# A hybrid decoder trunk on one core: the order of its first loads, and the queue of its first half's attention

## The chip, the core and the metric

The kernel runs on one core of a Trainium2 chip. The metric is the device time of one execution in microseconds (us); the median of three runs is taken. PE is the matmul engine (TensorE), DVE VectorE, ACT ScalarE, POOL GpSimd; SP issues nearly all DMAs.

## What is computed

Two layers over 1024 tokens of width 1024, float32. In each, a normalised input goes through one wide product, whose columns feed three groups: sparse attention (an indexer scores all causal keys, the 256 best per query stay), a conv module and a pool. Then an output product, an MLP of width 4096 with a squared ReLU, and a per-layer embedding behind a gate:

```python
a = rmsnorm(h, norm_mix_pre[i])
u = jnp.einsum('bsd,de->bse', a, w_in[i])
q, k, v, qi, ki, wi, u_conv, u_pool = jnp.split(u, IN_SPLITS, axis=-1)
...
mix = jnp.concatenate([y_attn, y_conv, y_pool], axis=-1)
mix = jnp.einsum('bse,ed->bsd', mix, w_out[i])
h = h + rmsnorm(mix, norm_mix_post[i])
m = rmsnorm(h, norm_mlp_pre[i])
m = jnp.square(jax.nn.relu(jnp.einsum('bsd,df->bsf', m, w_up[i])))
m = jnp.einsum('bsf,fd->bsd', m, w_down[i])
h = h + rmsnorm(m, norm_mlp_post[i])
gate = jax.nn.sigmoid(jnp.einsum('bsd,de->bse', h, ple_gate[i]))
h = h + gate * jnp.einsum('bsp,pd->bsd', p[i], ple_proj[i])
```

## The kernel before

Tokens are cut into two halves of 512, channels lie on the 128 partitions. The program goes through eight phases, for layer 0: the input product ("win") of the first half, win of the second, the rest ("m", `m_phase`) of the first half; then layer 1's win of the first half, layer 0's m of the second, and so on.

**Dense work.** A unit is one 128x512 output tile: eight input tiles by three matmuls, since float32 operands are split into a rounded part (hi) and its rest (lo): hi by hi (L255), hi by lo (L260), lo by hi (L261; a unit that goes first on new tiles has L257 and L258). Weights come by `weights` and `prepare` in the order of the list `coming`: a load of 512 KB by SP into wraw (two buffers, L211), ACT makes whi (L216), POOL wlo (L217). A unit's sums lie in pd (three buffers in PSUM) and are evacuated by ACT or DVE: L390 in win, L985 for the first four input tiles' worth of the first m.

**The start.** `first_x` (L1080 loads, L277 to L297) loads x and splits it into scaled hi and lo tiles on ACT and DVE, and squares it; the squares go through L319 (PE column sums), L347 (a power on POOL) and L324 (PE spreads the norm's factor, rb). `rope_tables` loads positions and constants, makes the rope tables on DVE and ACT, and sends them through DRAM. `first_x` of the second half runs at its own place in win of the first half, and its loads go into the buffer yT that the first half's x has used. The conv module's 31 taps are DVE steps of L586.

**Attention.** It is a generator that `run` advances between dense units, by a budget per phase. For a pair of heads and a block of 128 queries: PE scores (L647), DVE bias and maximum (L816), ACT exponential with its sum (L825), DVE reciprocal (L826), ACT scale (L827); then PE transposes (L839), ACT and DVE split the result (L272, L273), PE multiplies with the values (L847, L848), and `finish` (L853 to L862) stores into mixS in DRAM. `attend` keeps one group of heads ahead: a group's softmax is issued before the group ahead of it is weighted. The first half's blocks 2 and 3 take their tiles from the ring `rows`.

**The first half's m in layer 0** needs mixS whole. So its output product is in two parts: the four tiles of conv and pool first (L982 to L986), and when attention is through (`drain`), the four attention tiles (loaded at L970). A norm (`post_norm`: L319, L347, L324, then L925 and L926 for each tile, and new splits) leaves PE without tiles; it takes a filler, a part of the embedding's product (`embedding`, L954, evacuated at L956). The norm after the output product fills with output tiles 4 to 7, which are stored to DRAM (eS), and the norm after the MLP with tiles 0 to 3, which stay in SBUF for the gate.

A scheduler puts the instructions of each engine in order when the program is built, so a change in the code moves rows that it doesn't name. Engines run in order.

## Time and profile before

| | us |
|---|---|
| median of three runs | 2783.4 (2782.57 to 2784.98) |
| profiled execution | 2778.56 |
| its span in the trace | 2776.8 |
| PE busy | 2685.9 (97%) |
| DVE, ACT, POOL busy | 1660.4, 1588.5, 1348.8 |
| mean granted clock of PE | 0.994 |

All sums below stand against the profiled execution. PE is nearly always busy, so the stretches to look at are those in which it isn't: windows of the trace give them. A granted clock of 1.00 is 2.4 GHz, the higher of PE's two levels; a mean of 0.79 over a stretch is part of it at the lower, 1.2 GHz.

### The profile page before, as it was taken

To read this page: it belongs to the slowest core of one execution; us is meant where nothing else is said; L and a number is where in the kernel's file an instruction comes from. 1 tells how busy PE (TensorE), PEld (TensorE's weight loads), DVE (VectorE), ACT (ScalarE), POOL (GpSimd) and SP (SyncE) were. 2 spreads that over 40 slices of the span, in tenths; PEclk is the share of its full clock that TensorE was granted. 3 is DMA by queue.
4 is the path that set the end of the run, shared out by engine and by line. 5 is a ranking of instruction groups with operands and counts; after the bars stand their busy time and mean duration, and the time that the engine had idled before them with its cause. 6 is when DMAs were issued, how large, how long until landed. Compare 5 with 4: busy or idle time off the path is not lost.

```text
span 2776.8 us, 37158 instructions
## 1 busy us (share of the span) xinstructions
PE 2685.9 (97%) x12496; PEld 2210.5 (80%) x12496; DVE 1660.4 (60%) x3393; ACT 1588.5 (57%) x2971; POOL 1348.8 (49%) x1073
## 2 busy tenths in 40 slices
PE   8899999999999999999999999999999999999998
PEld 6778778887888777788888778788878887788886
DVE  6978578678557868784522585676785662311123
ACT  5357767766767434684733434677657764443343
POOL 4654334444334664544344765444443345544446
PEclk9999999999999999999999999999999999999999
DMA  5677554432344555644233646534222454422323
GB/s 183 199 196 220 134 165 120 107 99 84 88 110 124 195 188 186 183 122 118 90 100 109 222 141 222 158 97 112 98 88 84 103 185 152 141 94 96 99 95 132
DMA packets 192022, 377.41 MB, mean 136 GB/s; under 512 B 17432, under 2 KB 76952, under 8 KB 191832
## 3 DMA queue, kind: packets, MB, share of 16 engines
q1 hardware_dynamic: 130200, 319.46, 36.1%
q0 software_dynamic: 42240, 20.98, 4.6%
q10 hardware_dynamic: 19392, 34.61, 3.6%
q8 instruction: 98, 1.61, 0.2%
q14 instruction: 92, 0.75, 0.1%
HBM read 304.67 MB, written 70.32 MB: 135 GB/s over the span
## 4 chain that ended last, share of the span: by engine, by line
PE 77%; DVE 10%; DMA 6%; issue 2%; ACT 2%; POOL 2%; SPq 0%; ACTq 0%; POOLq 0%; DVEq 0%
PE pd L255 22%; PE pd L261 21%; PE pd L260 21%; PE bank L647 6%; DMA wraw<-win 2%; PE bank L839 2%; DVE bank L586 1%; POOL wlo L217 1%; PE bank L848 1%; PE bank L847 1%; DVE dtmp L925 1%; DVE row L801 1%; DMA kd<-kS 1%; DVE slot L273 1%; PE pd L319 1%
## 5 line engine op out<-in xcount | busy, mean ns | idle before, releaser
L217 POOL TENSOR_TENSOR wlo<-wraw,whi 128x512 fp32r<-128x512 f32 x824 | 1087.9, 1325 | 1211.7 <-ACT whi L216 1162.5
L255 PE MATMUL pd<-slot,whi 128*128 128x512 f32 x3296 | 1300.6, 395 | 38.4 <-ACT whi L216 17.8
L261 PE MATMUL pd<-slot,wlo 128*128 128x512 f32 x3168 | 1239.0, 392 | 12.7 <-POOL wlo L217 12.6
L260 PE MATMUL pd<-slot,whi 128*128 128x512 f32 x3168 | 1240.3, 392 | 0.4 <-DVE slot L278 0.3
L216 ACT ACTIVATE whi<-wraw 128x512 fp32r<-128x512 f32 x824 | 511.8, 628 | 767.3 <-PE pd L260 536.9
L255 PEld LDWEIGHTS pd<-slot,whi 128*128 128x128 f32 x3296 | 621.4, 189 | 177.1 <-ACT whi L216 22.2
L261 PEld LDWEIGHTS pd<-slot,wlo 128*128 128x128 f32 x3168 | 597.1, 188 | 139.7 <-POOL wlo L217 17.2
L260 PEld LDWEIGHTS pd<-slot,whi 128*128 128x128 f32 x3168 | 597.6, 189 | 119.7 <-DVE slot L278 1.2
L647 PE MATMUL bank<-kd,qst 128*128 128x512 f32 (+3 forms) x1024 | 259.1, 359 | 12.9 <-DVE mxc L816 5.0
L695 DVE SCALAR_TENSOR_TENSOR idx<-bank,wiT,idx 128x512 f32<-128x512 f32 (+3 forms) x300 | 187.7, 651 | 66.1 <-ACT bank L691 62.1
L647 PEld LDWEIGHTS bank<-kd,qst 128*128 128x128 f32 x1024 | 176.2, 189 | 48.4 <-DVE idx L695 10.5
L1012 DVE TENSOR_SCALAR pd<-pd 128x512 f32<-128x512 f32 x128 | 88.9, 696 | 170.3 <-PE pd L261 169.2
L691 ACT ACTIVATE bank<-bank 128x512 f32<-128x512 f32 (+2 forms) x320 | 153.2, 506 | 61.2 <-PE bank L647 59.1
L1031 DVE TENSOR_TENSOR yT<-yT,pd 128x512 f32<-128x512 f32 x96 | 65.4, 684 | 201.1 <-PE pd L261 201.0
L718 DVE TENSOR_SCALAR_CACHE_REDUCE row<-row,cc 128x640 f32<-128x640 uint16 (+1 forms) x124 | 133.6, 1078 | 72.2 <-ACT row L732 65.1
L586 DVE SCALAR_TENSOR_TENSOR bank<-win,vec,bank 128x512 f32<-128x512 f32 x232 | 164.3, 747 | 5.8 <-ACT bank L584 4.0
L732 ACT ACTIVATE row<-row,cc 128x768 f32<-128x768 uint16 (+1 forms) x124 | 121.4, 982 | 21.9 <-DVE cc L738 20.5
L273 DVE TENSOR_TENSOR slot<-pd,slot 128x512 fp32r<-128x512 f32 x128 | 87.8, 687 | 69.0 <-ACT slot L272 68.6
L297 DVE TENSOR_TENSOR dtmp<-dtmp,pd 128x512 f32<-128x512 f32 x88 | 60.2, 684 | 105.2 <-ACT pd L293 105.0
L816 DVE CUSTOM_DVE_ANT_0 row<-bank,idx 128x512 f32<-128x512 f32 (+3 forms) x160 | 92.1, 591 | 51.5 <-PE bank L647 38.5
L273 DVE TENSOR_TENSOR cmat<-bank,cmat 128x512 fp32r<-128x512 f32 (+1 forms) x160 | 98.3, 631 | 33.2 <-ACT cmat L272 32.4
L825 ACT ACTIVATE row<-row,nmc,rq 128x384 f32<-128x384 f32 (+5 forms) x96 | 93.0, 969 | 22.7 <-DVE nmc L821 18.4
(218 smaller groups left out, 2635.9 us busy)
## 6 DMA issues: line engine op xcount, KB each, us to landing
wraw<-wup SPq DMA_DIRECT2D x128, 512.0 KB
wraw<-wdown SPq DMA_DIRECT2D x128, 512.0 KB
wraw<-win SPq DMA_DIRECT2D x84, 512.0 KB
qiS<-dtmp ACTq DMA_DIRECT2D x64, 256.0 KB
slot<-mixS SPq DMA_DIRECT2D x32, 512.0 KB
wraw<-wgate SPq DMA_DIRECT2D x32, 512.0 KB
qst<-qiS POOLq DMA_DIRECT2D x48, 256.0 KB, 3.4
hS<-yT SPq DMA_DIRECT2D x48, 256.0 KB
```

Of the source, the lines that this page charges most:

```text
L216: sc.activation(hi, r, AF.Copy)
L217: gp.tensor_tensor(lo, r, hi.bitcast(F32), op=OP.subtract)
L255: te.matmul(ps, wh, xh, start=i == 0, stop=False)
L260: te.matmul(ps, wh, xl, start=False, stop=False)
L261: te.matmul(ps, wl, xh, start=False, stop=i == n - 1)
L273: ve.tensor_tensor(lo, src, hi.bitcast(F32), op=OP.subtract)
L586: ve.scalar_tensor_tensor(acc[:, c] if k == TAPS - 1 else pa, src, w, pa, op0=OP.mult, op1=OP.add)
L647: te.matmul(ps[:, :n1 - n0], q, kd[:, k, k0 + n0:k0 + n1], start=k == 0, stop=k == 1)
L691: sc.activation(r, r, AF.Relu)
L695: ve.scalar_tensor_tensor(at, r, w, at, op0=OP.mult, op1=OP.add)
L718: ve.tensor_scalar(flags[:, :Ws[j]], of[j], t, None, op0=op, op1=OP.add, accum_out=dst[:, j:j + 1])
L732: sc.activation(flags[:, :Ws[j]], of[j], AF.Sign, scale=-1.0, bias=c[:, j:j + 1], accum_out=cnt[:, j:j + 1])
```

## The change

1. **First loads.** The first weights are asked for ahead of the first x tile and the second ahead of the second x tile (before: one, after two x tiles); the constants cv go behind the rope's. For the second half a copy of eight columns of the first half's norm factor into yT is written ahead of its loads, so that they have to wait for it.
2. **Attention queue.** For the first half, blocks 2 and 3 use six tiles instead of rows' own (three of `rows` beside three of `spare`), and two groups are kept ahead instead of one. A generator that finds no free tile now gives way (`take`) instead of failing. In layer 0, block 3's scale goes from ACT to DVE. `drain` advances the other generators where its own gives way.
3. **Embedding.** In layer 0's first half the product of output tiles 0 to 3 (24 matmuls, four evacuations, four stores) stands after the first part of the output product, that is beside the end of attention, instead of in the norm after the MLP, which now has no filler; the gate reads these four tiles from eS, as it does the others.

```diff
@@ -109,6 +109,12 @@
...
+    def take(ring):
+        while not ring.free:
+            yield None
+        return ring.get()
@@ -153,7 +159,6 @@
...
     cv = const.tile([P, 2, 17], F32, name="cv")
-    sy.dma_start(cv, cinv)
     lent = dtmp.get()
@@ -189,6 +194,7 @@
...
         sy.dma_start(fr, invf)
+        sy.dma_start(cv, cinv)
         sy.dma_start(pf.bitcast(I32), at)
@@ -226,13 +232,14 @@
...
             if (l, hf) == (0, 0):
-                coming += [wout[l, o][:, 4:] for o in range(NK)] + [wout[l, o][:, :4] for o in range(NK)]
+                coming += [wout[l, o][:, 4:] for o in range(NK)] + [wple[l, i] for i in range(2)] + [wout[l, o][:, :4] for o in range(NK)]
             else:
                 coming += [wout[l, o] for o in range(NK)]
-            coming += [wple[l, i] for i in range(2, 4)]
+            apart = (l, hf) == (0, 0)
+            coming += [wple[l, i] for i in (range(2, 4) if apart else range(2, 4))]
             for gr in range(4):
                 coming += [wup[l, gr * 8 + u] for u in range(8)] + [wdown[l, gr, o] for o in range(NK)]
-            coming += [wple[l, i] for i in range(2)] + [wgate[l, o] for o in range(NK)]
+            coming += [wple[l, i] for i in (() if apart else range(2))] + [wgate[l, o] for o in range(NK)]
     ready = []
@@ -364,7 +371,7 @@
...
-        rb = rms_sb(sq, keep=rq[:, l, hf, 0])
+        rb = state["rb"] = rms_sb(sq, keep=rq[:, l, hf, 0])
         for i, f in ((1, 0.125), (2, -0.125)):
@@ -573,7 +580,7 @@
...
-        at = rows.get()
+        at = yield from take(rows)
         acc = at[:, :1024].rearrange("p (c t) -> p c t", c=2)
@@ -809,7 +816,7 @@
...
             for g in heads:
-                t = ring.get()
+                t = yield from take(ring)
                 mx, nm, rs, ri = tiny("mx", 2), tiny("nm", 1), tiny("rs", 1), tiny("ri", 1)
@@ -824,7 +831,11 @@
...
                 ve.reciprocal(ri, rs)
-                sc.activation(s, s, AF.Copy, scale=ri)
+                if l == 0 and b == 3:
+                    ve.tensor_scalar(s, s, ri, None, op0=OP.mult)
+                else:
+                    sc.activation(s, s, AF.Copy, scale=ri)
                 out.append(t)
@@ -862,11 +873,11 @@
...
-        def attend(some, at, ring):
+        def attend(some, at, ring, ahead=1):
             n = (some[-1] + 1) * P
-            before = None
-            for step in [(kv, b, g) for kv in range(2) for b in some for g in (0, 2)] + [None]:
+            queue = []
+            for step in [(kv, b, g) for kv in range(2) for b in some for g in (0, 2)] + [None] * ahead:
                 if step:
@@ -877,8 +888,9 @@
...
                         qst.put(q)
-                if before:
-                    (bkv, bb, bg), bpr = before
+                    queue.append((step, pr))
+                if len(queue) > ahead or not step:
+                    (bkv, bb, bg), bpr = queue.pop(0)
                     v0 = 4 * bkv if hf == 0 else 0
@@ -888,14 +900,19 @@
...
                         yield 2.0
-                before = step, pr
...
             yield from together(select(), attend(blocks[:2], (HALF, HALF), ctmp))
-            yield from attend(blocks[2:], (0, HALF), rows)
+            mine = []
+            for _ in range(3):
+                mine.append((yield from take(rows)))
+            spare.put(*mine)
+            yield from attend(blocks[2:], (0, HALF), spare, 2)
+            rows.put(*mine)
         else:
@@ -939,6 +956,8 @@
...
         ts = slice(hf * HALF, hf * HALF + HALF)
+        if not pairs:
+            return lambda: iter([None])
         pl = [slots.get() for _ in range(2)]
@@ -984,6 +1003,9 @@
...
+            for _ in embedding(l, hf, range(2), None)():
+                pass
             load(xs, range(4), ts)
@@ -999,7 +1021,7 @@
...
             yield 5.2
-        fill = embedding(l, hf, range(2, 4), None)
+        fill = embedding(l, hf, range(2, 4) if apart else range(2, 4), None)
         slots.put(*xs)
@@ -1036,7 +1058,7 @@
...
         es = []
-        fill = embedding(l, hf, range(2), es)
+        fill = embedding(l, hf, () if apart else range(2), es)
         xs, _ = post_norm(sqy, vl[:, V_MLP_POST:V_MLP_POST + 8], ts, hS, None, fill, apart2)
@@ -1075,11 +1097,14 @@
...
         xs = []
+        if hf == 1:
+            ve.tensor_copy(yT[:, :, :1], state["rb"][:, :NK].unsqueeze(2))
         for k in range(NK):
             h = yT[:, k]
+            if hf == 0 and k in (0, 1):
+                ready.append(prepare(coming.pop(0)))
             sy.dma_start(h, xT[k * P:(k + 1) * P, ts])
-            if k == 1 and hf == 0:
-                ready.append(prepare(coming.pop(0)))
         for k in range(NK):
@@ -1122,8 +1147,9 @@
...
-        while advance([x for x in bg if x[0] == (l, hf)]) is not None:
-            pass
+        while any(x[0] == (l, hf) for x in bg):
+            if advance([x for x in bg if x[0] == (l, hf)]) is None:
+                assert advance(bg) is not None
```

SP's first instructions, before (vec and cv are constants, yT x, wraw weights):

```order
L154 DMA vec<-vecs 128x204
L156 DMA cv<-cinv 128x34
L1080 DMA yT<-xT 128x512 x2
L211 DMA wraw_91<-win 128x1024
L1080 DMA yT<-xT 128x512 x6
L211 DMA wraw_92<-win 128x1024
L191 DMA fr<-invf 128x2
L513 DMA row_121<-wcp 128x256
L1080 DMA yT<-xT 128x512 x3
L211 DMA wraw_91<-win 128x1024
L1080 DMA yT<-xT 128x512 x4
L192 DMA dtmp_108<-pos 128x1x64
```

and after:

```order
L160 DMA vec<-vecs 128x204
L217 DMA wraw_91<-win 128x1024
L1107 DMA yT<-xT 128x512
L217 DMA wraw_92<-win 128x1024
L1107 DMA yT<-xT 128x512 x7
L196 DMA fr<-invf 128x2
L197 DMA cv<-cinv 128x34
L520 DMA row_121<-wcp 128x256
L217 DMA wraw_91<-win 128x1024
L217 DMA wraw_92<-win 128x1024
L198 DMA dtmp_108<-pos 128x1x64
L210 DMA tabS<-dtmp_108 128x64 x2
L217 DMA wraw_91<-win 128x1024
```

The weights stand behind vec alone, cv behind the x tiles, and of the second half's eight loads (the second mention of yT) the first stands behind five weights and the positions.

ACT around the last evacuations that stand beside attention in the first half's m, before (L985 evacuates the output product, L825 is an exponential, L827 a scale, L272 a split, L856 `finish`):

```order
L216 ACTIVATE whi_96<-wraw_92 128x512
L985 ACTIVATE yT<-pd_139 128x512
L272 ACTIVATE cmat_117<-bank_144 128x512
L272 ACTIVATE cmat_119<-bank_140 128x512
L825 ACTIVATE row_124,rsc_1356<-row_124,nmc_1352,rq 128x384
L825 ACTIVATE row_122,rsc_1357<-row_122,nmc_1353,rq 128x384
L827 ACTIVATE row_124<-row_124,ric_1360 128x384
L272 ACTIVATE cmat_115<-bank_144 128x512
L827 ACTIVATE row_122<-row_122,ric_1361 128x384
L825 ACTIVATE row_121,rsc_1358<-row_121,nmc_1354,rq 128x384
L825 ACTIVATE row_123,rsc_1359<-row_123,nmc_1355,rq 128x384
```

and after (L1004 is the evacuation of before's L985, L975 the embedding's, L832 the exponential, L838 the scale):

```order
L279 ACTIVATE cmat_119<-bank_141 128x512
L832 ACTIVATE row_122,rsc_1359<-row_122,nmc_1355,rq 128x384
L832 ACTIVATE row_121,rsc_1360<-row_121,nmc_1356,rq 128x384
L975 ACTIVATE dtmp_102<-pd_139 128x512
L838 ACTIVATE row_122<-row_122,ric_1363 128x384
L838 ACTIVATE row_121<-row_121,ric_1364 128x384
L222 ACTIVATE whi_94<-wraw_92 128x512
L975 ACTIVATE dtmp_108<-pd_137 128x512
L279 ACTIVATE cmat_115<-bank_140 128x512
L832 ACTIVATE idx_132,rsc_1357<-idx_132,nmc_1353,rq 128x512
L832 ACTIVATE idx_133,rsc_1358<-idx_133,nmc_1354,rq 128x512
L867 ACTIVATE ctmp_113<-bank_142 64x512
```

Before, eight exponentials (four of 384 columns, and four of 512 further on) follow the last L985; after, four of 512 follow the last L975, two of them behind these rows, and no scale of 512 is left on ACT in this place.

PE at the norm after the first half's MLP in layer 0, before (twelve transposes, the filler's first six matmuls, column sums L319, scores L647):

```order
L839 MATMUL bank_141<-ident,row_123 128x128
L255 MATMUL pd_139<-slot_85,whi_95 128x512
L260 MATMUL pd_139<-slot_85,whi_95 128x512
L261 MATMUL pd_139<-slot_85,wlo_99 128x512
L255 MATMUL pd_139<-slot_86,whi_95 128x512
L260 MATMUL pd_139<-slot_86,whi_95 128x512
L261 MATMUL pd_139<-slot_86,wlo_99 128x512
L319 MATMUL pd_138<-ones,dtmp_101 128x1 x4
L647 MATMUL bank_144<-kd,qst_128 128x512 x2
L847 MATMUL bank_142<-cmat_117,vst 128x256
```

and after (L850 is a transpose, L326 the column sums, L654 scores, L858 and L859 the values):

```order
L850 MATMUL bank_141<-ident,row_122 128x128
L850 MATMUL bank_141<-ident,row_121 128x128
L326 MATMUL pd_139<-ones,dtmp_105 128x1 x4
L654 MATMUL bank_144<-kd,qst_128 128x512 x2
L858 MATMUL bank_142<-cmat_117,vst 128x256
L326 MATMUL pd_139<-ones,dtmp_103 128x1 x4
L859 MATMUL bank_142<-cmat_118,vst 128x256
L858 MATMUL bank_142<-cmat_117,vst 128x256
L859 MATMUL bank_142<-cmat_118,vst 128x256
```

The column sums follow the transposes at once; there is no matmul of the embedding here.

## Rows read from the trace of the kernel before

**Rows 1.** The page's busy table: busy us, share of the span, instructions.

```profile
PE 2685.9 (97%) x12496; PEld 2210.5 (80%) x12496; DVE 1660.4 (60%) x3393; ACT 1588.5 (57%) x2971; POOL 1348.8 (49%) x1073
```

**Rows 2.** Windows: busy us of each engine, granted clock, DMA share, GB/s.

```profile
core 0: us, PE busy (x) PEld busy (x) DVE busy (x) ACT busy (x) POOL busy (x), PEclk, DMA share, GB/s
0.00:30.50 30.50, 17.79 (x72) 13.19 (x73) 22.85 (x41) 21.93 (x38) 13.17 (x16) 1.00 0.74 252
...
79.50:141.00 61.50, 53.66 (x230) 42.73 (x229) 57.55 (x80) 25.12 (x45) 40.37 (x33) 0.97 0.61 191
...
270.00:326.30 56.30, 55.28 (x271) 45.81 (x270) 31.70 (x83) 39.21 (x82) 23.79 (x20) 1.00 0.48 131
326.30:351.20 24.90, 19.61 (x103) 16.39 (x102) 15.75 (x47) 21.61 (x46) 2.82 (x3) 0.79 0.59 107
...
842.30:858.80 16.50, 16.50 (x109) 14.97 (x108) 11.57 (x30) 13.73 (x26) 4.94 (x4) 1.00 0.25 80
```

**Rows 3.** Timeline of SP: start us, us, engine, line, operation.

```profile
1.20 0.42 SPq L156 DMA_DIRECT2D cv<-cinv  x1
...
2.60 0.43 SPq L211 DMA_DIRECT2D wraw<-win  x1
```

**Rows 4.** Timeline of PE at the start; in brackets the wait and its releaser.

```profile
9.36 0.79 PE L255 MATMUL pd<-slot,whi 128*128 128x512 f32 x1 [9.36 <-ACT whi L216]
...
28.41 0.51 PE L255 MATMUL pd<-slot,whi 128*128 128x512 f32 x1 [1.85 <-ACT whi L216]
...
30.12 0.50 PE L261 MATMUL pd<-slot,wlo 128*128 128x512 f32 x1 [0.98 <-POOL wlo L217]
```

**Rows 5.** Timeline of DVE, 25 to 50 us.

```profile
27.33 0.74 DVE L278 SCALAR_TENSOR_TENSOR slot<-yT,vec,slot 128x512 fp32r<-128x512 f32 x1
...
48.36 0.70 DVE L390 TENSOR_TENSOR pd<-pd,rb 128x512 f32<-128x512 f32 x1 [6.79 <-PE pd L261]
```

**Rows 6.** Waits of PE, 79 to 141 us: us, times, longest.

```profile
PE pd L261 <- POOL wlo L217: 2.8, 1, 2.8
```

**Rows 7.** Timeline of PE at the end of the first attention.

```profile
326.30 0.28 PE L847 MATMUL bank<-cmat,vst 128*128 128x256 f32 x1
326.42 0.60 PE L839 MATMUL bank<-ident,row 128*128 128x128 f32 x4
326.78 0.36 PE L848 MATMUL bank<-cmat,vst 128*128 128x256 f32 x1
...
343.91 1.54 PE L839 MATMUL bank<-ident,row 128*128 128x128 f32 x6 [1.94 <-ACT row L827]
...
351.15 0.28 PE L848 MATMUL bank<-cmat,vst 128*128 128x256 f32 x1
```

**Rows 8.** Chain of work that ended last, 350 to 364 us.

```profile
358.32 5.10 DMA slot<-mixS
```

**Rows 9.** Groups by line and form: count, busy us, mean ns, idle.

```profile
L956 ACT ACTIVATE dtmp<-pd 128x512 f32<-128x512 f32 x32 | 18.8, 591 | 3.2 <-PE pd L261 3.1
...
L825 ACT ACTIVATE row<-row,nmc,rq 128x512 f32<-128x512 f32 x16 | 12.9, 806 | 0.1
...
L827 ACT ACTIVATE row<-row,ric 128x512 f32<-128x512 f32 x16 | 11.1, 711 | 0.3 <-DVE ric L826 0.2
```

**Rows 10.** Timeline of DVE, the scalar step L800 on 128x512.

```profile
268.18 1.60 DVE L800 TENSOR_SCALAR idx<-idx,thrc 128x512 f32<-128x512 f32 x1
...
1256.63 0.48 DVE L800 TENSOR_SCALAR idx<-idx,thrc 128x512 f32<-128x512 f32 x1
```

**Rows 11.** Timeline of POOL, 262 to 271 us.

```profile
266.96 3.97 POOL L217 TENSOR_TENSOR wlo<-wraw,whi 128x512 fp32r<-128x512 f32 x3 [6.16 <-ACT whi L216]
```

**Rows 12.** Timeline of PE at the norm after the MLP.

```profile
840.73 0.39 PE L261 MATMUL pd<-slot,wlo 128*128 128x512 f32 x1
...
842.09 0.40 PE L261 MATMUL pd<-slot,wlo 128*128 128x512 f32 x1
...
853.52 0.60 PE L324 MATMUL pd<-ident,rrn 128*128 128x128 f32 x4
...
858.84 0.39 PE L255 MATMUL pd<-slot,whi 128*128 128x512 f32 x1
```

## The prediction

> **What bounds the kernel now.** I read the page's busy table first [rows 1]: TensorE (PE) is busy 97% of the span. Dense matmuls stand 0.227 us apart where nothing is in the way (840.73 to 842.09, six steps) [rows 12], so PE time that is really work can't shrink by this change (it has as many matmuls after as before), and time can come only out of the stretches in which PE waits. The windows by stage [rows 2] show where these lie inside the change's reach: the first 30.5 us (PE busy 17.8), 79.5 to 141 (53.7 of 61.5), the end of layer 0's first attention with nothing else left to do, 326.3 to 351.2 (19.6 of 24.9, at a mean granted clock of 0.79). The stretch 842.3 to 858.8, the second norm of the first half, is full (16.5 of 16.5). The change fills the third of these, and takes its filler from the last. The busy shares count overlapping matmuls, so below I count waits by start times: PE work is priced at its undisturbed spacing, 0.2275 us for a dense matmul, and the same for a 512-column L647, 0.36 for four transposes of L839 (326.42 to 326.78), 0.12 for a matmul of L847 or L848 (326.30 to 326.42) [rows 7].
>
> **Part 1, the order of the first loads.** Before, SP issues vec, cv and two of the x tiles ahead of the first weights, which it issues at 2.60 us [rows 3]; ACT turns them into whi, and that releases PE's first matmul at 9.36 [rows 4]. After, the weights stand behind vec alone, where cv stood, at 1.20: 1.4 us earlier, and with 104 + 512 KB ahead of their end instead of 1,145 KB (estimate from the tiles' sizes). I take 1.5 us for the first matmul. The x tiles after it come no later in the list, and ACT sets their pace in both. Further, PE's order now interleaves the first two units tile by tile, so it has 48 dense matmuls to run before it needs the norm, and the third unit's weights are asked for earlier: the waits at 28.41 (1.85 us) and 30.12 (0.98) [rows 4], 2.8 together, lie on the path, since the third unit is next. I take 2.5 of them, so 4.0 for the first 30.5 us, between 1.5 (the first matmul only) and 5.5 (also the time that PE stood in single-column sums of L319).
>
> Held back: a copy of the first half's norm into yT makes the second half's eight loads wait for it. Its price: SP is in order, and behind the waiting load stand the next weights and the rope tables. On DVE six splits of the second half now stand ahead of the evacuation at 48.36; that row waited 6.79 us for PE, and six times 0.74 us is 4.4 [rows 5], so they fit with 2 us to spare. I cost them at nothing; with that cover gone it would be up to 4.4 us of DVE, minus the 2.8 below. Rope's eight small DVE steps now stand ahead of the norm's two, on data whose load is issued behind four of the weights, so this too can be late. These are the reasons for the low end of 1.5.
>
> The conv chain on DVE (L586), whose first step follows the evacuation at 48.36 and the units behind it, begins earlier if the start is 4 us earlier, and of the 7.8 us that PE does not work in 79.5 to 141 [rows 2] (DVE busy 57.6 of 61.5) some 0 to 2.8 us go (2.8: the wait for wlo there [rows 6]); I take 1. Part 1: **5.0**, between 1.5 and 8.3.
>
> **Part 2, the deeper queue and the scale on DVE.** In the tail, from the end of PE's last dense matmul (326.30, the first of the rows) to its last L848 (351.15, so 351.27) there are 102 attention matmuls: 40 L839, 44 of L847/L848, 12 L647 of 512 columns, six shorter. At the spacings above: 3.6 + 5.3 + 2.8 + 0.9 = 12.6. So 12.4 of 25.0 us are waits, and the longest that is named is softmax's: L839 for ACT's scale L827, 1.94 us at 343.91 [rows 7]. Eight heads have their exponential still to come after ACT's last dense evacuation: **1.55 us of wait each**. After, the order puts 24 embedding matmuls ahead of the tail and, by the third group in flight, eight more heads' exponentials ahead of their evacuations: four heads, all of 512, are left. The tail has 90 attention matmuls: 32 L839, 40 L847/L848, 14 L647, 4 short: 2.9 + 4.8 + 3.2 + 0.3 = 11.2. With 4 × 1.55 = 6.2 of waits it lasts 17.4. It begins 24 × 0.2275 = 5.5 and 12.6 − 11.2 = 1.4 later, at 333.2, and ends at 350.6, 0.7 earlier than before, with 5.5 us of dense work done besides: 6.2 in all. From it goes what the four heads cost beside dense work: the dense stretch 270 to 326.3 holds eight heads and lost 2.1 us (its length less the spacings of its 271 matmuls [rows 2]), 0.26 a head, so 1.0. What follows the tail, finish, store and load of mixS (the load 5.10 us [rows 8]), is the same in both, and with it PE's work there on the next index. Part 2: **+5.1**.
>
> Bounds: the four heads' waits may fall to 4 × 0.26 (then part 2 is 12.4 − 1.0 − 1.0 = 10.4), or all twelve last heads may pay 1.55 (below). Engines beside it: ACT was busy 39.2 of 56.3 us in the dense stretch [rows 2]; four more exponentials of 0.81 and four evacuations of 0.59 [rows 9] make 44.8 of 63: enough. The scale of the eight 512-column heads goes from ACT (0.71 [rows 9]) to DVE. No such step of DVE is in the trace; the nearest is L800, a scalar step on 128x512 in SBUF, 0.48 us at 1256.63 and 1.60 at 268.18 [rows 10], where POOL was in three of L217 from 266.96 on [rows 11]. I take 0.6, near the shorter, since POOL has little to do in the tail. DVE was busy 31.7 of 56.3 and 15.8 of 24.9 [rows 2], so it is not the bound, and exponential, reciprocal and scale of one head stay in series: no gain by itself but ACT's 0.71 between two heads.
>
> The Trainium skill, SBUF — State Buffer, section Who interferes with whom, speaks against this move: a tensor_scalar in a two-port mode and GpSimd lock each other out of a shared port pair for a whole instruction, and who issues first wins. The long L800 beside POOL's L217 [rows 10, 11] agrees with it; by the rule at its worst the sum is rival C's, by the shorter row the forecast's.
>
> **Part 3, the norm that loses its filler.** Between the last dense matmul of wdown (842.09) and the first that needs the normalised tiles (858.84) PE ran 24 embedding matmuls, 5.5 us, and 11 us of attention and sums, without a gap [rows 12]. After, the 24 are gone and the order there reads transposes, sums, scores. The norm's chain (L319, POOL's power, L324 at 853.52, L925, L926, splits on DVE) doesn't get shorter by itself: if it takes 16.5 us still, the 5.5 are given back whole. But DVE was busy only 11.6 of the 16.5 [rows 2], and idle for 4.9; with PE's queue shorter, L319 comes 1.4 us sooner at once (six dense matmuls stood ahead of it). I let half of the 4.9 close: cost 5.5 − 2.5 = **3.0**, between 0.6 and 5.5. Four more e tiles now come from DRAM for the gate, loads issued a norm ahead: nothing. [...]
>
> **Sum.** 5.0 + 5.1 − 3.0 = 7.1 us. The profiled run took 2778.56 (span 2776.8) and by that would take 2771.5; it lies 4.8 under the median of the three runs, 2783.4, and I carry the difference to the median: **2776.3**. A measurement of this kernel tells about 0.2%, 5.6 us, from no change, so faster means under 2777.8.
>
> **Rivals.**
> A, the filler was not needed and the tail closes: four heads at 0.26, norm 0.6, start 5.0: 10.4 + 5.0 − 0.6 = 14.8, 2768.6. For it: DVE and ACT have idle time in both. Against it: softmax's steps are in series and the last group has nothing behind it.
> B, given back: the norm costs all of 5.5 and the start brings only 2 (the conv chain on DVE, nearly unbroken, ends when it did): 5.1 + 2 − 5.5 = 1.6, 2781.8. For it: DVE's 57.6 of 61.5 us in 79.5 to 141, and L925/L926 in series behind L324.
> C, the scale on DVE is slow: each stands behind POOL, 1.6 instead of 0.48. Four in the tail are 4.5 us: 7.1 − 4.5 = 2.6, 2780.8. Against it: in the tail POOL is busy 2.8 of 24.9 us [rows 2]. It is the mechanism of the rule that the Trainium skill has in SBUF — State Buffer, section Who interferes with whom.
> D, slower: threading twelve heads' transposes into dense work holds PE, which is in order, at each: 12 × 1.55 = 18.6 of waits instead of 12.4. With the norm's 5.5 and a start of 4: −6.2 − 5.5 + 4 = −7.7, 2791.1. It decides where ACT and DVE can't finish a group's exponentials within the dense matmuls that the order puts between it and its transposes; against it ACT's 44.8 of 63.
> E, the change doesn't do what it says: the held-back loads stall SP and the second half's first units wait, so the start gives nothing; with the rest as forecast 5.1 − 3.0 = 2.1, 2781.3. I count it with B.
>
> **How the numbers follow.** Forecast 0.55, A 0.13, B and E 0.17, C 0.05, D 0.10. The forecast's own range, from the ends that are likely of each term, is 2773 to 2780; four fifths of it lie under 2777.8. Faster: 0.8 × 0.55 + 0.13 = 0.57. Slower: D but for a fifth, 0.08. Same: 0.35. The range that leaves no more than 2 in 10 out takes in A's time, nearly, and B, C and E: 2767 to 2784; D is left out.
>
> **What would show it.** PE's first matmul at about 7.8, and the first matmul on wlo of its third unit by about 26 to 26.5 instead of 30.1; the conv chain's first step some 4 us earlier. The tail 17 us long, from 333 less the start's gain, with no wait above 2 us in the dense stretch before it, and the wait for mixS as long as before. A gap of about 3 us between L319 and the first matmul on normalised tiles in the norm, with L324 less than 11.4 us after the end of wdown. The prediction is wrong if that norm loses 5 us or more, if L839 waits for the scale amid dense matmuls, or if the second half's loads are waited for near 48.

## The result

| | us | |
|---|---|---|
| before, median of 4 runs | 2784.2 | 2782.6 to 2788.8 |
| changed, median of 4 runs | 2770.2 | 2768.9 to 2772.1 |
| ratio | 0.9944 | 95% interval 0.9932 to 0.9956 |
| forecast | 2776.3 | 2767 to 2784 |

The change is 14 us faster (by the interval 12 to 19), twice the 7.1 that the forecast had, and inside its range. A second comparison gave 0.9956 (0.9942 to 0.9970). The profiled execution of the change has a span of 2770.3 us, 6.5 less than that of before (2776.8); which of the two differences is to be believed was the first question for the runs. Three executions that lie far above the others of their kernels (3100, 7788 and 12488 us) are left out of all comparisons. Lines have moved: a dense unit is now L262, L267, L268; whi L222, wlo L223; column sums L326, spread L331; transposes L850, exponential L832, scale L838 and L836, values L858 and L859.

The page of the changed kernel, busy table and chain:

```profile
PE 2685.5 (97%) x12496; PEld 2213.7 (80%) x12496; DVE 1656.6 (60%) x3402; ACT 1584.7 (57%) x2963; POOL 1351.9 (49%) x1073
...
PE 82%; DVE 9%; DMA 4%; issue 2%; ACT 1%; POOL 1%; SPq 0%; ACTq 0%; POOLq 0%; DVEq 0%
```

PE's work is what it was [rows 1]; its waits are less. To see where, I took from each trace the time from every PE matmul's start to the next one's, less the median spacing of its form, and summed these waits over stretches cut at equal amounts of PE work. The stretches are named by their times in the profile of before. Two profiles stand for each kernel, the second ones from the runs below; the last column compares the means.

| stretch, us | what | before, twice | changed, twice | waits saved |
|---|---|---|---|---|
| 0 to 136 | start and first units | 28.0, 26.8 | 27.3, 28.3 | −0.4 |
| 136 to 283 | rest of both halves' win, layer 0 | 6.5, 7.0 | 4.8, 5.0 | 1.9 |
| 283 to 417 | end of the first attention | 22.4, 22.8 | 18.1, 18.1 | 4.5 |
| 417 to 854 | MLP | 7.0, 7.1 | 7.3, 6.9 | 0 |
| 854 to 929 | norm and gate | 4.9, 5.1 | 4.3, 4.3 | 0.7 |
| 929 to 1084 | first half's win, layer 1 | 14.7, 16.4 | 11.0, 9.5 | 5.3 |
| 1084 to end | the rest | 58.7, 58.6 | 63.3, 62.2 | −4.1 |

Down to 1084 us the change saves 12.0 us. Behind that it loses 4.1 in the profiles. PE's order differs from that of before only up to 1399 us, and the loss lies behind it, among rows that stand in the same order; this last stretch lost 58.0 to 63.3 us in the kernels of this study. The 1.9 us of 136 to 283 are no firmer: the other kernels made from the change lose 5.6 to 8.2 there. I don't put these 4.1 us down to the change; why the stretch differs so stays open. What is left by the profiles is 7.9 us, and why the medians of the plain runs lie 14 us apart stays open too.

**The start.** PE at the start of the changed kernel (start us, us, engine, line; in brackets the wait and its releaser):

```profile
7.30 0.79 PE L262 MATMUL pd<-slot,whi 128*128 128x512 f32 x1 [7.30 <-ACT slot L284]
...
25.36 0.75 PE L331 MATMUL pd<-ident,rq 128*128 128x128 f32 x4 [2.13 <-POOL rq L354]
27.88 0.80 PE L262 MATMUL pd<-slot,whi 128*128 128x512 f32 x1 [1.76 <-DVE dtmp L280]
28.47 0.63 PE L267 MATMUL pd<-slot,whi 128*128 128x512 f32 x1
28.89 0.63 PE L268 MATMUL pd<-slot,wlo 128*128 128x512 f32 x1
```

The first matmul comes 2.1 us earlier than in [rows 4]; what it waits for is now ACT's split of the first x tile, no longer the weights. The third unit starts at 27.88 and not at about 25: it doesn't wait for its weights any more, but for an evacuation. From 27.88 to 32.3 matmuls stand 0.43 us apart instead of 0.23. The windows there (the last three figures are granted clock, DMA share and GB/s):

```profile
22.00:27.80 5.80, 1.99 (x10) 1.11 (x9) 2.60 (x13) 3.73 (x8) 2.12 (x2) 0.83 0.05 11
27.80:33.00 5.20, 5.12 (x13) 4.12 (x14) 1.35 (x5) 0.80 (x2) 1.40 (x2) 0.54 0.93 294
```

PE had little to do for 5 us, and then ran at a granted clock of 0.54, most of it at the lower level of 1.2 GHz. What held the norm is on DVE, SP and ACT:

```profile
22.00 0.18 DVE L199 CAST dtmp<-dtmp 128x64 f32<-128x64 int32 x1
...
23.75 0.20 DVE L205 TENSOR_SCALAR dtmp<-dtmp 128x64 f32<-128x64 f32 x1
23.86 0.15 DVE L336 TENSOR_SCALAR rvd<-pd 128x4 f32<-128x4 f32 x1
```

```profile
19.01 0.77 SPq L198 DMA_DIRECT2D dtmp<-pos  x1
```

```profile
24.02 1.28 ACT L206 ACT_TABLE_LOAD   x1 [5.57 <-DVE rvd L336]
25.32 0.26 ACT L206 ACTIVATE dtmp<-dtmp 128x64 f32<-128x64 f32 x1
```

The positions are loaded only at 19.0 (by SP's waits the load stood 6.5 us for a dtmp tile that the sum of the squares, L304, still used). Rope's eight steps stand ahead of the norm's L336, which so comes 1.9 us later on DVE. ACT, idle for 5.57 us, then loads its table for the sines ahead of the first units' evacuation at 26.52.

**The end of the first attention.** PE there; the first two rows are the last dense matmul and what follows, the last is the output product going on:

```profile
331.23 0.39 PE L268 MATMUL pd<-slot,wlo 128*128 128x512 f32 x1
331.46 1.07 PE L654 MATMUL bank<-kd,qst 128*128 128x512 f32 x4
...
338.55 0.39 PE L858 MATMUL bank<-cmat,vst 128*128 128x256 f32 x1 [2.04 <-ACT cmat L279]
...
350.94 0.29 PE L859 MATMUL bank<-cmat,vst 128*128 128x256 f32 x1
...
362.88 0.50 PE L262 MATMUL pd<-slot,whi 128*128 128x512 f32 x1 [3.25 <-DMA slot<-mixS]
```

From 331.46 to 351.06 the tail lasts 19.6 us, 11.2 of them work and 8.4 waits, against 12.4 of 25.0 before [rows 7]. No transpose waits for the scale any more. By the spacings of the table above the tail loses 4.0 us less and the rows behind it 0.5 less; the dense work ahead of it, with more heads threaded in, loses no more than before. The output product goes on at 362.88, 0.6 us before its old time, with the 24 embedding matmuls done; in the kernel before it is this row:

```profile
363.47 0.80 PE L255 MATMUL pd<-slot,whi 128*128 128x512 f32 x1 [2.67 <-DMA slot<-mixS]
```

The new DVE step, all eight:

```profile
L836 DVE TENSOR_SCALAR idx<-idx,ric x5: 485/486/487, 314.6 to 343.5; 128x512 f32<-128x512 f32 x5
L836 DVE TENSOR_SCALAR row<-row,ric x3: 485/486/492, 293.4 to 344.3; 128x512 f32<-128x512 f32 x3
```

**The norm without its filler:**

```profile
841.07 0.40 PE L268 MATMUL pd<-slot,wlo 128*128 128x512 f32 x1
841.30 1.47 PE L850 MATMUL bank<-ident,row 128*128 128x128 f32 x12
842.61 0.95 PE L326 MATMUL pd<-ones,dtmp 128*128 128x1 f32 x8
...
849.14 0.60 PE L331 MATMUL pd<-ident,rrn 128*128 128x128 f32 x4
...
853.00 0.33 PE L850 MATMUL bank<-ident,row 128*128 128x128 f32 x1 [0.72 <-DVE mxc L823]
853.09 0.48 PE L262 MATMUL pd<-slot,whi 128*128 128x512 f32 x1
```

From the last matmul of wdown to the first on new tiles it is 12.0 us instead of 16.75 [rows 12]: the 5.5 us of filler are gone and 0.7 us of wait has come. The last step of DVE ahead of the spread, before and after:

```profile
850.09 0.17 DVE L349 TENSOR_TENSOR rrn<-rrn,r2d 128x4 f32<-128x4 f32 x1
```

```profile
847.75 0.15 DVE L356 TENSOR_TENSOR rrn<-rrn,r2d 128x4 f32<-128x4 f32 x1
```

Before, the spread (853.52) starts 3.3 us behind it, with seven of the filler's matmuls (1.6 us) started in between on PE; after, 1.2 us. Six more (1.4 us) stood ahead of the column sums.

### The profile page after: what moved, and what is told of

Read it like the earlier page. It is cut to its first block, busy times and chain, and to the rows that moved or that the text cites. A ratio compares the mean times of both kernels' runs of the same rounds, so it can differ in the third digit from the quotient of the medians.

```text
span 2770.3 us, 37169 instructions
## 1 busy us (share of the span) xinstructions
PE 2685.5 (97%) x12496; PEld 2213.7 (80%) x12496; DVE 1656.6 (60%) x3402; ACT 1584.7 (57%) x2963; POOL 1351.9 (49%) x1073
## 4 chain that ended last, share of the span: by engine, by line
PE 82%; DVE 9%; DMA 4%; issue 2%; ACT 1%; POOL 1%; SPq 0%; ACTq 0%; POOLq 0%; DVEq 0%
PE pd L262 24%; PE pd L268 23%; PE pd L267 23%; PE bank L654 6%; PE bank L850 2%; DVE bank L593 1%; PE bank L859 1%; PE bank L858 1%; POOL wlo L223 1%; DVE dtmp L942 1%; DMA dtmp<-tabS 1%; PE pd L265 1%; DMA wraw<-win 1%; PE pd L326 1%; DVE idx L702 1%
## 5 line engine op out<-in xcount | busy, mean ns | idle before, releaser
L223 POOL TENSOR_TENSOR wlo<-wraw,whi 128x512 fp32r<-128x512 f32 x824 | 1090.9, 1328 | 1217.5 <-ACT whi L222 1179.9
L262 PE MATMUL pd<-slot,whi 128*128 128x512 f32 x3296 | 1301.4, 395 | 39.9 <-ACT slot L284 11.3
L268 PE MATMUL pd<-slot,wlo 128*128 128x512 f32 x3168 | 1240.1, 393 | 5.7 <-POOL wlo L223 5.7
L267 PE MATMUL pd<-slot,whi 128*128 128x512 f32 x3168 | 1242.2, 392 | 0.0
L222 ACT ACTIVATE whi<-wraw 128x512 fp32r<-128x512 f32 x824 | 513.4, 629 | 768.1 <-PE pd L267 562.0
L262 PEld LDWEIGHTS pd<-slot,whi 128*128 128x128 f32 x3296 | 622.6, 189 | 178.9 <-ACT slot L284 14.7
L268 PEld LDWEIGHTS pd<-slot,wlo 128*128 128x128 f32 x3168 | 598.4, 189 | 131.3 <-POOL wlo L223 7.7
L267 PEld LDWEIGHTS pd<-slot,whi 128*128 128x128 f32 x3168 | 599.1, 189 | 120.1 <-DVE slot L285 1.0
L654 PE MATMUL bank<-kd,qst 128*128 128x512 f32 (+3 forms) x1024 | 257.2, 358 | 11.3 <-DVE mxc L823 3.8
L654 PEld LDWEIGHTS bank<-kd,qst 128*128 128x128 f32 x1024 | 176.6, 189 | 44.8 <-DVE idx L702 7.9
L739 ACT ACTIVATE row<-row,cc 128x768 f32<-128x768 uint16 (+1 forms) x124 | 121.5, 982 | 22.8 <-DVE cc L745 21.5
L304 DVE TENSOR_TENSOR dtmp<-dtmp,pd 128x512 f32<-128x512 f32 x88 | 60.3, 686 | 103.3 <-ACT pd L300 102.9
L823 DVE CUSTOM_DVE_ANT_0 row<-bank,idx 128x512 f32<-128x512 f32 (+3 forms) x142 | 81.5, 588 | 41.0 <-PE bank L654 35.1
L279 ACT ACTIVATE cmat<-bank 128x512 fp32r<-128x512 f32 (+1 forms) x160 | 83.8, 547 | 17.0 <-PE bank L850 13.4
```

The costliest lines, as they stand in the source:

```text
L222: sc.activation(hi, r, AF.Copy)
L223: gp.tensor_tensor(lo, r, hi.bitcast(F32), op=OP.subtract)
L262: te.matmul(ps, wh, xh, start=i == 0, stop=False)
L267: te.matmul(ps, wh, xl, start=False, stop=False)
L268: te.matmul(ps, wl, xh, start=False, stop=i == n - 1)
L654: te.matmul(ps[:, :n1 - n0], q, kd[:, k, k0 + n0:k0 + n1], start=k == 0, stop=k == 1)
```

## The experiments

Times are medians; a ratio is to the runs of before on the same chip, with its 95% interval. The last two columns are waits of one profile, in the stretches 283 to 417 and 929 to 1084 of the table above; heads are those whose exponential follows ACT's last dense evacuation in the first attention. The runs were made on four chips, so two kernels other than before are best compared by their ratios. The profiled execution is one of its kernel's runs and can lie off their median: that of before again by 4 us, of one group ahead by 5.6 and of tables on ACT by 4.2, all three on the quick side.

| run | us | ratio | heads | 283 to 417 | 929 to 1084 |
|---|---|---|---|---|---|
| before again | 2784.2 | 1.0005 (0.9992 to 1.0019) | 8 | 22.8 | 16.4 |
| change again | 2770.3 | 0.9956 (0.9942 to 0.9970) | 4 | 18.1 | 9.5 |
| start undone | 2772.9 | 0.9965 (0.9953 to 0.9978) | 4 | 17.2 | 12.3 |
| start alone | 2788.5 | 1.0023 (1.0011 to 1.0035) | 8 | 24.3 | 14.1 |
| scale on ACT | 2773.0 | 0.9957 (0.9942 to 0.9973) | 4 | 18.6 | 12.8 |
| filler back | 2779.2 | 0.9983 (0.9968 to 0.9998) | 6 | 17.9 | 17.8 |
| one group ahead | 2776.5 | 0.9968 (0.9955 to 0.9981) | 4 | 18.8 | 8.2 |
| no holding back | 2776.8 | 0.9974 (0.9964 to 0.9983) | 4 | 17.7 | 11.2 |
| filler back, stored | 2781.2 | 0.9985 (0.9969 to 1.0001) | 6 | 18.7 | 18.5 |
| rope's other tile | 2765.9 | 0.9930 (0.9911 to 0.9949) | 4 | 18.0 | 10.5 |
| tables on ACT | 2776.9 | 0.9977 (0.9963 to 0.9991) | 8 | 21.2 | 14.5 |
| six tiles alone | 2782.1 | 0.9997 (0.9983 to 1.0011) | 6 | 20.4 | 14.4 |

### Both kernels again

> The kernel before, unchanged, against itself. The medians of the two kernels lie 14.0 us apart (2784.2 and 2770.2), their profiled executions only 6.5 (spans 2776.8 and 2770.3). If the profiled execution of before was by chance a quick one, a new profile of it gives a span of 2780 to 2785, and shows in which stretch the further 4 to 8 us lie. If the profile is typical and the medians of four runs were off, its span is again 2775 to 2779 and its median here near 2779. The ratio is 1.000 within 0.2% either way.

> The changed kernel, unchanged, on the same chip as the other runs. By the medians of before it is 12 to 16 us faster than before, ratio 0.9943 to 0.9957; by the two profiled executions 6.5 us, ratio 0.9977.

The medians repeat: 2784.2 and 2770.3, 14 us apart, ratio 0.9956. The second profile of before has a span of 2778.2, near the first, and the profiles' spans differ by 6.5 to 9.7 us, not 14: neither case of the expectation held whole. Both profiled executions of before are quicker than most of its runs, and no profile shows what the slower ones lose. The runs of before spread widely (2772 to 2789 in 32, 2776 to 2795 in 12), those of the change little (2768 to 2776). Where one profile of before differs from the other is in the first half's win of layer 1: the wait at 1010 us below is 3.18 us in one and 0.3 in the other.

### The start

The edit that undoes it (and, the other way round on the kernel before, makes it alone):

```diff
     cv = const.tile([P, 2, 17], F32, name="cv")
+    sy.dma_start(cv, cinv)
...
         sy.dma_start(fr, invf)
-        sy.dma_start(cv, cinv)
...
-        if hf == 1:
-            ve.tensor_copy(yT[:, :, :1], state["rb"][:, :NK].unsqueeze(2))
         for k in range(NK):
             h = yT[:, k]
-            if hf == 0 and k in (0, 1):
-                ready.append(prepare(coming.pop(0)))
             sy.dma_start(h, xT[k * P:(k + 1) * P, ts])
+            if k == 1 and hf == 0:
+                ready.append(prepare(coming.pop(0)))
```

> The change with its first part (order of the first loads, copy that holds the second half's input back) undone. By the forecast's terms the start is worth 5.0, so this run is 5 us slower than the change. By the two profiles the start is worth nothing: by 50 us the changed kernel is 0.5 us behind in waits, since its norm waits behind rope's steps on DVE; then this run is within 2 us of the change, or 1 us faster. If the start is what lies behind the 14 us, it is 8 us or more slower.

> The kernel before with the first part of the change alone. By the forecast's terms 5 us faster than before (ratio 0.9982); by the two profiles the same as before within 2 us up to 140 us of the program, and at most 2 faster by 270; if the start is behind the 14 us, 8 us or more faster (0.9971 or below).

Undone, the change loses 2.5 us by the medians, which the two intervals don't tell apart from nothing. In waits down to 136 us it loses 29.8, the change 27.3 and 28.3. Alone on the kernel before, the start makes it slower, by 3 to 10 us, which no case of the expectation had. Its start itself isn't worse (27.4 us of waits down to 136, 26.8 and 28.0 before). The largest piece of the loss that I can name is far from it, one row behind 690 us:

```profile
695.38 0.44 PE L647 MATMUL bank<-kd,qst 128*128 128x128 f32 x2 [3.97 <-DVE mxc L816]
```

Before, the same row waits 0.63 us at 688.12. The order of the scores among the dense work has moved there, and DVE comes to them only after the long selection steps. The run with one group ahead (3.97 again) and the one with six tiles alone (3.98) have this wait too, the change and the others don't. So the row is a loss that a new order can bring; that it is all of this run's loss isn't shown.

The copy alone taken away:

```diff
-        if hf == 1:
-            ve.tensor_copy(yT[:, :, :1], state["rb"][:, :NK].unsqueeze(2))
```

> The change without the copy that holds the second half's x loads back, the other order of the first loads kept. If holding back is what makes the changed start worth its 2.5 us against the change with the start undone, this run is 2 us slower than the change or more; if it is what keeps the start from gaining (splits of the second half ahead of the evacuation on DVE), 1 to 4 us faster. Part 1 without it is the first matmul at 7.3 us instead of 9.36, by itself 2 us.

6.5 us slower than the change by the medians, 5 by the ratios, and 5.1 us more of waits down to 136 us: it is the holding back that makes the new order of loads bearable, though the ratios' intervals overlap a little. Without it DVE runs five splits of the second half ahead of the norm, and PE's spread waits 5.88 us:

```profile
22.07 4.40 DVE L285 SCALAR_TENSOR_TENSOR slot<-yT,vec,slot 128x512 fp32r<-128x512 f32 x5
26.39 0.18 DVE L199 CAST dtmp<-dtmp 128x64 f32<-128x64 int32 x1
26.50 0.15 DVE L336 TENSOR_SCALAR rvd<-pd 128x4 f32<-128x4 f32 x1
```

```profile
29.18 1.11 PE L331 MATMUL pd<-ident,rq 128*128 128x128 f32 x4 [5.88 <-POOL rq L354]
```

Then the scratch of rope in another tile, on the change:

```diff
-        ropes = dtmp.get()
+        ropes = ctmp.get()
...
-        dtmp.put(ropes)
+        ctmp.put(ropes)
```

> The change with the rope tables' scratch in a ctmp tile instead of the dtmp tile that the last square of x also uses. In the change the positions' load waits on SP until 19.0 us for that tile, rope's steps on DVE run 22.0 to 23.9, ahead of the norm's, and ACT's table load and sines hold its first evacuation until 26.5. Here the load goes at about 11 and rope's steps fall between the squares; the norm's spread comes 1.5 to 2 us earlier, the third unit 2.5 to 3.5 us earlier (24.4 to 25.4 instead of 27.9): the term of 4.0 that the forecast gave to the first 30 us. Total 2 to 4 us under the change, if the conv chain on DVE lets it through; the same as the change, if that chain sets the time to 140 us.

This is the quickest version, 2765.9 us, 4.4 under the change by the medians and 7 by the ratios, whose intervals overlap a little. SP loads the positions at 9.66, and PE's rows become:

```profile
24.83 0.65 PE L331 MATMUL pd<-ident,rq 128*128 128x128 f32 x4 [1.13 <-POOL rq L354]
26.01 0.49 PE L262 MATMUL pd<-slot,whi 128*128 128x512 f32 x1 [0.53 <-DVE dtmp L280]
26.34 0.39 PE L267 MATMUL pd<-slot,whi 128*128 128x512 f32 x1
```

```profile
26.00:31.00 5.00, 4.99 (x22) 4.13 (x23) 1.31 (x4) 0.72 (x2) 2.18 (x3) 1.00 0.95 300
```

ACT's table load is out of the way (18.81), but rope's last step on DVE and the sines on ACT (23.44 to 24.2) are still ahead of the evacuation at 24.65, so the third unit starts 1.9 us earlier and not 2.5 to 3.5. But PE's granted clock stays at 1.00, and 22 matmuls go in 5.0 us where the change has 13 in 5.2. Together the waits to 32 us fall from 16.7 and 17.0 in the change to 13.0; in the two profiles of before they are 16.7 and 16.2.

### The queue, the scale and the filler

The scale back on ACT, and one group ahead:

```diff
-                if l == 0 and b == 3:
+                if False:
```

```diff
-            yield from attend(blocks[2:], (0, HALF), spare, 2)
+            yield from attend(blocks[2:], (0, HALF), spare, 1)
```

> The change with block 3's scale back on ACT. The forecast gave the move nothing by itself but ACT's 0.71 us between two heads: 0 to 3 us slower than the change (2770 to 2773), the loss in the tail of the first attention. If the scale on DVE is what shortens the tail's waits, 4 us or more slower; if it stands behind POOL, faster than the change.

> The change with one group of heads kept ahead instead of two, its six tiles kept. The forecast's reason is that eight heads' exponentials follow the last dense evacuation again: four more heads at 1.55 less 0.26 each in the tail, 5 us slower than the change. If the embedding alone covers the tail, 0 to 2 us slower.

The scale's place isn't told apart from nothing (2.6 us by the medians, on another chip; the ratios, 0.9957 and 0.9956, are the same), as forecast. With one group ahead the end of the attention is nearly that of the change (18.8 us of waits, four heads left); the total is 6 us above it by the medians and 3 by the ratios, whose intervals overlap. Where it loses isn't shown: its profiled execution has the 3.97 us of the row behind 690 us and is still as quick as the change's (2770.8). So a second group ahead is not what leaves four heads; my expectation of this run, eight heads again, was wrong.

The filler back in the norm, first as before, then with its tiles stored to eS:

```diff
-                coming += [wout[l, o][:, 4:] for o in range(NK)] + [wple[l, i] for i in range(2)] + [wout[l, o][:, :4] for o in range(NK)]
+                coming += [wout[l, o][:, 4:] for o in range(NK)] + [wout[l, o][:, :4] for o in range(NK)]
...
-            coming += [wple[l, i] for i in (() if apart else range(2))] + [wgate[l, o] for o in range(NK)]
+            coming += [wple[l, i] for i in range(2)] + [wgate[l, o] for o in range(NK)]
...
-            for _ in embedding(l, hf, range(2), None)():
-                pass
...
-        fill = embedding(l, hf, () if apart else range(2), es)
+        fill = embedding(l, hf, range(2), es)
```

```diff
-        fill = embedding(l, hf, range(2), es)
+        fill = embedding(l, hf, range(2), None if apart else es)
```

> The change with the embedding's 24 matmuls back in the norm after the MLP, the deeper queue and the scale kept. The forecast: the tail is 5.5 us less covered and the norm 3 us better, so 2 to 3 us slower than the change. By the two profiles the norm costs nothing without its filler (4.9 us of waits with, 4.2 without), so the whole cover counts: 5 to 6 us slower than the change, 2775 to 2776. If it is the changed order that saves 5 us of waits in the first half's win of layer 1 and this saving comes with the norm, it goes as well, and the run is 10 us slower, near before.

> The change with the embedding's 24 matmuls back in the norm after the MLP, as in the run with the filler back, but their tiles stored to eS and read again by the gate, as in the change. It tells the place of the filler from the four dtmp tiles that the old kernel keeps until the gate. If the kept tiles cost the waits in the first half's win of layer 1 (17.8 us with the filler back, 9.5 to 11.0 in the change), this run loses 10 to 11 us there and is at the change's 2770 to 2772. If the place does, through the order that the scheduler makes of SP's rows (two loads of weights ahead of the rope table's load instead of three), it stays near 2779: the order of SP there is that of the run with the filler back.

Back in the norm it costs 9 us by the medians (7.5 by the ratios), but at neither of the places that the forecast weighed: the end of the attention keeps 17.9 us of waits, and the stretch 854 to 929 is 5.1 instead of 4.3. The loss is in the first half's win of layer 1, the last case of the expectation: 17.8 instead of 9.5 to 11.0. Storing the tiles doesn't change it (18.5), so it isn't the four tiles that are kept.

And six tiles for blocks 2 and 3 with everything else as before (made from the changed kernel; `take` and the new `drain` stay in it):

> The kernel before with six tiles instead of four for block 2 and 3 of the first half's attention, one group ahead as before; start, scale and embedding as before. All runs with part of the queue's change undone keep a tail that is 3.5 to 5 us better than before (waits from 300 us of PE work to 360 and the stretch ahead: 17 to 19 instead of 22.5), whichever part is undone; what they share is the six tiles. If the tiles are what shortens the tail, its waits fall to 18 or 19 here too and L839 no longer waits for the scale L827. If it is the number of heads left after the last dense evacuation, as the forecast has it (1.55 us a head), six heads are left here by the order: 12.4 down to 9.3 in the tail itself, 20 to 21 in all. The total is 2780 to 2782, since SP's order in the first half's win of layer 1 is that of before, with its waits of 15 to 18 us.

With six heads left and one group ahead the waits are 20.4, between before and the change, as the count of heads would have it; but the two runs with the filler back have six heads as well, two groups ahead, and 17.9 and 18.7. With one group ahead the waits fall with the heads, 22.6, 20.4, 18.8 for eight, six and four, about 1 us a head; with two groups ahead six heads do as well as four, near 18. But kernels with the same eight heads have 21.2 to 24.3, so steps of 2 us are near what one count of heads gives by itself. What in particular shortens the waits from 20.4 to 18 stays open.

### Why the first half's win of layer 1 waits

In the second profile of before, SP (the L377 rows load rope's table, L211 weights), and then PE:

```profile
982.29 6.04 SPq L211 DMA_DIRECT2D wraw<-win  x2
1000.90 0.63 SPq L377 DMA_DIRECT2D dtmp<-tabS  x1
1001.63 0.39 SPq L211 DMA_DIRECT2D wraw<-win  x1
```

```profile
1010.05 0.39 PE L261 MATMUL pd<-slot,wlo 128*128 128x512 f32 x1
1013.62 0.80 PE L255 MATMUL pd<-slot,whi 128*128 128x512 f32 x1 [3.18 <-ACT whi L216]
1014.21 0.63 PE L260 MATMUL pd<-slot,whi 128*128 128x512 f32 x1
```

SP has issued two loads of weights, then stands from 988 to 1000.9 at the table's load (its waits name the store of qS out of the dtmp tile, 10.6 us), and the next weights go behind it. Their unit finds no whi for 3.18 us, and its next matmul stands 0.59 us behind instead of 0.23. In the first profile of before SP stands nearly as long (989.6 to 1000.4), but the same row waits only 0.32 us. In the change three loads stand ahead of the table's:

```profile
976.39 15.28 SPq L217 DMA_DIRECT2D wraw<-win  x3
993.61 3.84 SPq L384 DMA_DIRECT2D dtmp<-tabS  x2
```

The order of SP with the filler back, stored or not, is that of before: two, then the table. It divides all profiles but one: from 992 to 1016 us, the six of kernels with two loads ahead of the table's (before twice, start alone, six tiles alone, filler back, stored) lose 3.2 to 9.7 us of waits, the seven of kernels with three 0.4 to 1.4. All with two have the filler in the norm, all with three have it moved. To see whether the stand does it, only the table's loads were moved, on the kernel before:

```diff
-                    sy.dma_start(x[a:a + 8 * n], tabS[i][:, ts].unsqueeze(1).broadcast_to([8, n, HALF]))
+                    (sc if (l, hf) == (1, 0) else sy).dma_start(x[a:a + 8 * n], tabS[i][:, ts].unsqueeze(1).broadcast_to([8, n, HALF]))
```

> The kernel before with the rope table's loads of the first half's win in layer 1 issued by ACT instead of SP, and nothing else. In a second profile of before SP stands from 988 to 1000.9 us at that load, which waits for a dtmp tile that is being stored, with weights behind it; PE then waits 3.2 us for them at 1010. If SP's stand is what costs before the 5 us that the change saves in this stretch, the waits there (14.7 and 16.4 us) fall to 10 to 12, and the run is 3 to 6 us faster than before. If the weights were late for another reason, or ACT's stand takes the place of SP's, it is the same or slower.

6 us faster than before (2 to 10 by the interval). SP now issues three loads from 977 to 1000, and from 992 to 1016 us, where the two profiles of before lose 3.3 and 8.2 us, it loses 2.6, of which 1.0 is one row that waits for DVE; no row waits 0.5 us for weights. But from 1029 to 1054 it loses 4.3 us, in rows that wait for DVE, ACT and wlo, where before lost 2.8 and 0.1, and the whole stretch has 14.5 us, not the 10 to 12 that were expected. (These times are those of before; the others are cut at the same PE work.) So the wait for weights near 1010 comes with SP's stand and goes with it, though the stand doesn't always cost as much; it is not all that the stretch loses. The profile's gain lies elsewhere (2.5 us less in the start and 1.4 in the attention, neither of which the edit names).

## Why the forecast was right, and where not

The time lies in the range and the sign is right, but with luck. Of the sum's four terms one came out near its size, the start and the conv chain brought nothing, the norm cost little, and the largest gain had no term. By the profiles, against which the sum was made, the change is 6.5 to 9.7 us faster, near the forecast's 7.1; by the medians 14. That is nearest to rival A (14.8, 2768.6), but of A only the norm held.

- **Start, +4.0 in the first 30 us: measured about 0.** The first matmul was right and more (7.30, forecast 7.8), and the third unit's waits for weights went, as forecast. The failed step is the sentence that rope's steps "can be late": it had no price but a low end of 1.5. They were late, because the positions' load waits for a tile of the squares. The norm's L336 came 1.9 us late, the evacuation stood behind the sines, and behind the idle time the granted clock was 0.54: ten spacings of 0.43 instead of 0.23 us cost 2.0, as much as the first matmul had won. The run with rope's other tile shows it: 3.9 us of waits less than the change and 3.5 less than before, near the 4.0 that the first 30 us were to bring. The held-back splits did fit ahead of the evacuation, but with less room than thought: the six took 6.58 us (42.99 to 49.57) instead of 4.4, and that row still waited 0.36 us for PE.
- **Conv chain, +1: not there.** Its first step is at 55.84, not earlier than before (55.21); with rope's other tile it is at 50.06, but the waits behind the start stay (10.9 there, 10.6 and 11.3 in the change).
- **Attention, +5.1: measured 4.5.** The size is right, its parts are not. The tail lasts 19.6 us and not 17.4: four heads waited 8.4 us, 2.1 each instead of 1.55, so the tail saves 4.0 and not 6.2. That is nearly made up because threading heads into the dense work cost nothing (forecast 1.0) and the rows behind the tail lose 0.5 less. Nor is the count of heads the whole reason: six heads do as well with two groups ahead. The filler's cover, 5.5 of the sum, is PE work wherever it stands, and moving it out of the norm and into this place shortens no wait here (17.9 with it back in the norm).
- **DVE's scale:** 0.486 us each, forecast 0.6. Rival C is out: the longest took 0.492. None of the eight began while POOL was in L223 by its rows, so the rule of the Trainium skill (SBUF — State Buffer, Who interferes with whom) wasn't tried on it. Rows of the run with rope's other tile agree with the rule: the scalar step L201 on 128x64, which takes 0.20 us in the change, took 1.30 with POOL in L223.

```profile
18.50 1.30 DVE L201 TENSOR_SCALAR ctmp<-ctmp 128x64 f32<-128x64 f32 x1
```

```profile
18.34 3.20 POOL L223 TENSOR_TENSOR wlo<-wraw,whi 128x512 fp32r<-128x512 f32 x2 [6.30 <-ACT whi L222]
```

- **Norm, −3.0: measured −0.7** (5.5 us of filler gone, 4.7 us shorter; −1.3 by the spacings of the table). The term was mis-sized: the forecast had 2.5 of the 5.5 us close, and 4.2 to 4.7 did. The spread came 7.8 us after the last matmul of wdown instead of 11.2 [rows 12]. The filler had hardly been hiding the norm's chain; eighteen of its matmuls, 4.1 us, stood in PE's order ahead of the spread. Behind the norm, from 860 to 878, the change loses 1.9 us less, which no term had, so the stretch 854 to 929 gains 0.7. Every kernel with the filler moved has this gain and none with the filler in the norm; through which rows isn't shown. Rival B's condition (5.5 given back) is out, A's (0.6) nearly holds.
- **The 5.3 us that no step had** come from the first half's win of layer 1. I had read that part of the order as moved and looked at none of its waits. With 4.5, 0.7, 1.9, 5.3 and −0.4 the change saves 12.0 down to 1084 us, and 7.9 in all with the last stretch.
- **Rivals D and E.** D, slower, had no sign: no row of PE waits between 315 and 331. E half had one: ACT did wait for the second half's loads (7.91 us until 36.51, 0.94 until 44.90), but PE has no wait between 30 and 60 us.
- **Slips in the working.** In SP's list the second x tile comes one place later than before, not "no later". Rival C counts each scale at 1.6 against 0.48, though the sum has 0.6 for it; against 0.6 it is 4.0 and not 4.5. Neither changes the forecast.

## What to carry to other kernels

Where a scheduler sets the order, an edit's own place holds only a part of its effect: here 5 of the 12 us saved down to 1084 us lay in a stretch whose code was not touched, and three variants got a new wait of 4 us in one row, over 300 us away from their edits. So read the order of the queues that wait (SP first) for all of the program, and cost a scratch tile's next owner as a wait: one shared tile held nearly all of the start's gain.

A filler in a norm is no cover for free: its matmuls stand in the queue ahead of the sums and the spread. Where other work fills the norm too, taking the filler out costs little (about 1 us here, for 5.5 us of matmuls). Whether it gains at its new place is another question: here it shortened no wait there, and the gain that went with it lay in SP's order 150 us on.

## What the runs showed of the hardware

A stretch of 5 us with little on PE (2.0 us busy from 22.0 to 27.8) was followed by a granted clock of 0.54 over the next 5.2 us; with rope's other tile, where the waits around the same four short matmuls are 1.1 and 0.5 us instead of 2.1 and 1.8, it stayed at 1.00 (26.0 to 31.0). Ten spacings of 0.43 instead of 0.23 us make 2.0 of the 3.9 us that this run brought, about as much as the shorter waits themselves.
